# The end of a mixture of experts: three last experts that write their own outputs, and a last norm that holds fewer slots

## The chip, the cores and the metric

The kernel runs on one core of a Trainium2 chip. The core has a matrix engine (PE), a vector engine (DVE), a scalar engine (ACT), GpSimd (POOL), and a sync engine (SP) that here only issues DMA transfers; POOL issues DMA too, the indirect ones (gathers and scatters by a list of rows), in a queue of its own. The engines run side by side, each through its own list of instructions in order, and wait for each other by semaphores. The metric is the device time of one launch in microseconds.

## The reference

One decoder layer, in float32, on 1024 tokens of 1024 channels: a token mixing (sparse attention and RWKV-7, merged), a cross-attention into 256 memory rows, and a grouped mixture of experts, each followed by a LayerNorm of `alpha * x + y`. Only the last part is touched, and the norms:

```
group = argmax over 4 groups of the sum of the two best scores in it
e_idx = the two best of the 4 experts of that group          # per token
gate  = their scores over the scores' sum
y     = sum over the token's two experts of gate * (silu(x @ w_gate[e]) * (x @ w_up[e])) @ w_down[e]
x     = layer_norm(alpha * x + y, ln3_g, ln3_b)               # eps 1e-5
```

There are 16 experts with `w_gate` and `w_up` of 1024 x 512 and `w_down` of 512 x 1024. With the given inputs an expert has between 108 and 160 tokens.

## The kernel before, in words

Up to about 1418 us of the profiled execution the kernel does the token mixing, the cross-attention and the router. Then come the experts, to about 1877 us.

**Products.** A float32 product is made of three: operands are split into a high part (`whi`, `exh`, `ehh`, made by ACT as a cast) and a low part (`wlo`, `exl`, `ehl`, the difference, made by DVE, for one weight chunk of four by POOL); then high x high, low x high and high x low are summed (`k.mm3`, L35 to L37). An expert's weights are six pieces of 1 MB: two of gate, of up, of down. A piece is loaded into one of six raw slots by SP (`load`, L1508), and its parts take one of six high and one of six low slots, all in rotation (`piece`).

**Lists.** The router writes, per expert, a list of slots: a token to read, a row to add to, a gate. The experts are ordered by their number of tokens; in this order the first eight have a main block of 128 slots and a remainder block of 64, the others a main block alone. An empty slot reads token 0 with gate 0, and adds to one of the 128 dump rows that follow the 1024 tokens' rows of the sum. A remainder's list is read twice, onto both halves of the partitions (`rows(..., twice=True)`).

**An expert** (`expert`, a generator whose stages `run` interleaves). Tokens are gathered by POOL (`gather`, L1540, `exg`), transposed by PE (`turned`, L1547, `etp`), and split. Then come gate (`w(0)`), up (`w(1)`) and down (`w(2)`), 24 matmuls of 512 columns each (down's in two halves of 12). A remainder's 64 tokens have high and low part side by side in the stationary operand (`exr`, `ehr`), so that they cost 16 matmuls more in each of gate, up and down (L1580, L1628, L1629), 16 small ones that add the halves and transpose (`etq`, L1599), and transposes of their own. The output goes through ACT (gate as scale, `ey`) and POOL adds its rows to the sum in DRAM (`accd`, `result`, L1621): one indirect transfer with add for a main block, two for a remainder. These transfers are in one order: an add waits for the add before it.

**The end.** The last `LATE` experts don't leave their tokens' outputs to others: each gathers the rows of the sum at its tokens (`z`, L1540 with `src=acc`), adds its own result (L1618), normalizes (`self.ln(z)`) and scatters it to the output (L1624), besides adding to the sum. Ahead of them, `tiles` (L1750ff) makes all 1024 outputs from the sum so far: it loads eight tiles of 128 tokens (L1757), takes moments (by DVE, L967 and L968, or by ACT, L961 and L962), 1/deviation on POOL (L969 or L963 adds eps, L970 raises to -1/2), scales and shifts (L976 and L981 on DVE, or L978 on ACT and L979 on POOL) and writes (L1763). The tiles take `HOLD` raw slots, two tiles each, and these slots hold no weights any more (`self.held`). Late outputs overwrite those of the tiles; the transfers to the output follow each other.

**Order.** `run` opens the experts in a mixed order: two with a remainder, then alternately one without and one with, then the rest without. A scheduler that works on a timeline of estimated durations sets each engine's order from the order of the program, which counts as priority. Steps in a row of the loop in `run` (L1709ff) belong to three experts: the tokens and gate of n, the down of n - 1, the tokens of n + 1.

Nothing follows but the loop `rest` for experts with more tokens than slots, which has no turn with these inputs.

Of the kernel before, what the change touches and what calls it, by code (L numbers as in the profile page):

```python
# [57 lines left out]
def load_xT(k, pool, ps, xin, ident, xh, xl, nt=NT, tag="xraw", bufs=3, pt=(("tp", 2),)):  # L58
    """four token tiles at a time: their loads, then their transposes"""
# [22 lines left out]
class Inproj:  # L82
    """x @ w_in; every consumer's layout goes to DRAM scratch."""
# [40 lines left out]
    # weights stationary, channels on the partitions  # L124
# [5 lines left out]
    def halves(self, wh, wl, evac, tag=None, marks=()):  # L130
        """a half of the tokens at a time"""
# [15 lines left out]
    def tokens(self, x, w, nh):  # L147
        """four token tiles by channels, from channels by tokens"""
        tp = self.bank(nh, "iptp")
        for i in range(4):  # L150
            self.k.nc.tensor.transpose(tp[:, w * i:w * i + w], x[:, 128 * i:128 * i + 128], self.ident[:w, :w])
        return tp[:, :4 * w]
# [112 lines left out]
def t5_onehot():  # L265
    """bucket of distance 1023 - i, one-hot (columns past distance 0 stay empty)"""
# [11 lines left out]
def bias_rows(k, pool, ev, ps, skew):  # L278
    """the bias by distance in DRAM, a copy for every partition; read with rows one place shorter, row p starts p places earlier"""
# [16 lines left out]
class Tables:  # L296
    """bias tables by distance: tb[p, h, c]: distance p + 896 - c; tcm: the compressed keys'; the window's far edge"""
# [24 lines left out]
def compress(k, cst, pool, ps):  # L322
    """k_cmp (twice on the partitions, in parts) and v_cmp (tokens on the partitions, in parts)"""
# [68 lines left out]
class Nsa:  # L392
    def __init__(self, k, cst, dp, skew, ps, keep, right):
        """first loads and the compressed branch's keys and values; ps: a pool with banks for that; keep: opens a pool that stays"""
# [33 lines left out]
    def load(self, t, g, half):  # L428
        """by halves of the tokens"""
# [10 lines left out]
    def attention(self):  # L440
# [6 lines left out]
        with tc.tile_pool(name="nq", reuse_waits="tile", bufs=1) as self.pq, tc.tile_pool(name="nw", reuse_waits="tile", bufs=2) as pw, tc.tile_pool(name="np", reuse_waits="tile", bufs=2, space=PSUM) as ps:  # L447
            def front(br, g, qt, t, st):
                """scores, softmax and gates of one tile of 128 queries of a group"""
# [28 lines left out]
            def weights(g, qt, sums, bs):  # L478
                """the gates over the sums"""
# [7 lines left out]
            def compressed(g, qt, t, st):  # L487
                """scores, softmax and gates against the compressed keys, four heads at once"""
# [20 lines left out]
            def back(g, qt, t, st):  # L509
                """all three branches into one sum: channels of four heads by queries"""  # L510
# [37 lines left out]
            def mix(a, na, b, nb):  # L548
                """steps of a among the first ones of b"""
# [71 lines left out]
class Rwkv:  # L621
    """RWKV-7 in chunks of 64 tokens; an item is a pair of heads and half of the tokens.

    Per chunk, with c the running sum of the log decay: al = e^{c_prev} kk, be = e^{-c} kk a, ka = e^{-c} k, rho = e^{c} r;
# [607 lines left out]
NREM = 8  # L1232
# [228 lines left out]
class Experts:  # L1461
# [193 lines left out]
    def run(self, px, ps):  # L1655
# [50 lines left out]
        for n in range(NE + 1):  # L1706
# [10 lines left out]
            if n + 2 < NE:  # L1717
                open_(n + 2)
# [183 lines left out]
```

## Time and profile before

| what | us |
| --- | --- |
| median of 3 runs | 1899.67 (1896.10 to 1902.39) |
| profiled execution, its span | 1889.9, mean granted clock 0.966 of full |
| experts, from their first gather to the last DVE instruction | about 1424 to 1877 |
| last remainder matmul ends | about 1815 |
| last matmul ends | about 1862 |
| last scatter issued | 1878.5 |
| end of the span | 1889.9 |

The profiled execution's span runs from its first to its last instruction; the median is of the whole launch, of other executions, and 9.8 us larger. In the rows below a busy time is the sum of an engine's instructions; bracketed times are idle time ahead of an instruction, with what ended it. PE's records overlap each other (a matmul of 512 columns is shown with 0.40 us, and one starts every 0.23 us).

### The profile page before, as it was taken

Reading aid. Unit: us, or ns where it says so; the run is one execution under the profiler, and the core shown is the slowest. Engines: PE = TensorE matmul, PEld = TensorE weight load, DVE = VectorE, ACT = ScalarE, POOL = GpSimd, SP = SyncE. Lnnn points to the kernel's source line nnn. Section 1 sums busy time; section 2 is a strip of 40 time slices with the busy share of each in tenths; the row PEclk is TensorE's granted clock in tenths of the full one; section 3 lists DMA queues with packets and bytes.
Section 4 is the critical chain, followed back from the end, with each engine's and each line's share of the span. In section 5 each row is a group of like instructions: output and inputs, shape, how many; then the busy total and the mean of one; then the engine's idle time right before and its main releaser. Section 6 shows DMA issues by size and latency. Waiting matters only on the chain. (4 is left out here: it accounts for less than half of the span.)

```text
span 1889.9 us, 27421 instructions
## 1 busy us (share of the span) xinstructions
PE 1763.5 (93%) x9206; PEld 1433.0 (76%) x9206; DVE 1323.7 (70%) x2774; ACT 849.3 (45%) x1742; POOL 670.3 (35%) x756
## 2 busy tenths in 40 slices
PE   8999999999999999999999899999998999999992
PEld 6877777777788887877888577878796887787771
DVE  3225886888887512498987675557888788788876
ACT  4223313434333222287876341034415676666662
POOL 1123202221222122155445122100356665666556
PEclk9999999999999999999999999999989999999996
DMA  7363343444332227702101774033326999899984
GB/s 232 110 186 106 116 162 113 140 122 126 101 113 84 67 89 231 256 9 82 40 9 32 236 221 167 23 98 126 137 84 246 310 331 289 278 295 292 320 269 143
DMA packets 246144, 302.00 MB, mean 160 GB/s; under 512 B 54653, under 2 KB 142741, under 8 KB 245488
## 3 DMA queue, kind: packets, MB, share of 16 engines
q1 hardware_dynamic: 238016, 273.59, 44.7%
q0 software_dynamic: 7984, 26.62, 5.7%
q8 instruction: 74, 1.21, 0.3%
q14 instruction: 70, 0.57, 0.1%
HBM read 234.05 MB, written 70.98 MB: 161 GB/s over the span
## 5 line engine op out<-in xcount | busy, mean ns | idle before, releaser
L1518 DVE TENSOR_TENSOR wlo<-wraw,whi 128x512 fp32r<-128x512 f32 x288 | 274.5, 1000 | 34.9 <-ACT whi L1517 33.9
L35 PE MATMUL acc<-xh,wh 128*128 128x512 f32 (+1 forms) x656 | 273.0, 416 | 5.2 <-ACT wh L117 3.0
L37 PE MATMUL acc<-xh,wl 128*128 128x512 f32 (+1 forms) x656 | 267.0, 408 | 0.1
L36 PE MATMUL acc<-xl,wh 128*128 128x512 f32 (+1 forms) x656 | 267.1, 408 | 0.0
L1517 ACT CAST whi<-wraw 128x512 fp32r<-128x512 f32 x384 | 207.4, 621 | 36.5 <-PE eacc L1580 10.1
L118 POOL TENSOR_TENSOR wl<-wraw,wh 128x1024 fp32r<-128x1024 f32 (+1 forms) x41 | 104.0, 2536 | 304.1 <-ACT wh L117 259.8
L35 PEld LDWEIGHTS acc<-xh,wh 128*128 128x128 f32 (+1 forms) x656 | 125.0, 191 | 44.0 <-issue 6.8
L1518 POOL TENSOR_TENSOR wlo<-wraw,whi 128x512 fp32r<-128x512 f32 x96 | 138.8, 1476 | 49.4 <-ACT whi L1517 38.1
L37 PEld LDWEIGHTS acc<-xh,wl 128*128 128x128 f32 (+1 forms) x656 | 124.8, 190 | 33.8 <-issue 5.1
L36 PEld LDWEIGHTS acc<-xl,wh 128*128 128x128 f32 (+1 forms) x656 | 125.2, 191 | 30.0 <-issue 3.2
L840 DVE TENSOR_TENSOR tinv<-xinv,ln 128x248 f32<-128x248 f32 (+30 forms) x248 | 85.5, 345 | 40.5 <-DMA ln<-ld 24.3
L28 DVE TENSOR_TENSOR pl<-ptp,ph 128x512 fp32r<-128x512 f32 (+1 forms) x148 | 98.3, 681 | 11.6 <-ACT ph L28 11.1
L470 ACT ACTIVATE pp<-pp,nm 128x640 f32<-128x640 f32 (+7 forms) x128 | 94.2, 738 | 16.4 <-DVE nm L469 15.6
L28 ACT CAST ph<-ptp 128x512 fp32r<-128x512 f32 (+1 forms) x148 | 84.7, 582 | 26.6 <-PE ptp L523 23.6
L36 PE MATMUL eacc<-wlo,exh 128*128 128x512 f32 x240 | 94.2, 393 | 0.4 <-DVE wlo L1518 0.4
L35 PE MATMUL eacc<-whi,exh 128*128 128x512 f32 x240 | 94.3, 393 | 0.0
L37 PE MATMUL eacc<-whi,exl 128*128 128x512 f32 x240 | 94.1, 392 | 0.0
L841 DVE TENSOR_TENSOR xinv<-xinv,tinv 128x248 f32<-128x248 f32 (+30 forms) x248 | 87.6, 353 | 5.9
L475 POOL TENSOR_SCALAR pp<-pp,wgt 128x640 f32<-128x640 f32 (+7 forms) x128 | 88.9, 717 | 1.0
L969 POOL TENSOR_SCALAR lnrs<-lnmv 128x1 f32<-128x1 f32 x21 | 19.6, 934 | 181.0 <-DVE lnmv L968 173.1
L523 PE MATMUL ptp<-ident,pp 128*128 128x128 f32 x528 | 82.1, 278 | 0.3 <-DVE pl L28 0.3
L117 ACT CAST wh<-wraw 128x1024 fp32r<-128x1024 f32 (+1 forms) x41 | 42.2, 1030 | 81.8 <-PE acc L36 44.4
(498 smaller groups left out, 4476.2 us busy)
## 6 DMA issues: line engine op xcount, KB each, us to landing
wraw<-in_moe_w_up SPq DMA_DIRECT2D x32, 1024.0 KB
wraw<-in_moe_w_gate SPq DMA_DIRECT2D x32, 1024.0 KB
wraw<-in_moe_w_down SPq DMA_DIRECT2D x32, 1024.0 KB
wraw<-in_w_in SPq DMA_DIRECT2D x40, 512.0 KB
sm<-ev SPq DMA_DIRECT2D x32, 256.0 KB
sr<-ev SPq DMA_DIRECT2D x28, 256.0 KB
skew<-skew SPq DMA_DIRECT2D x1, 4608.0 KB
xraw<-in_x SPq DMA_DIRECT2D x8, 512.0 KB
```

What stands on the lines that cost most here:

```text
L28: x = nc.scalar.copy(hi, src), nc.vector.tensor_tensor(lo, src, hi.bitcast(F32), ALU.subtract)
L35: nc.tensor.matmul(out, ah, bh, start=start, stop=False)
L36: nc.tensor.matmul(out, ah, bl, start=False, stop=False)
L37: nc.tensor.matmul(out, al, bh, start=False, stop=stop)
L118: nc.gpsimd.tensor_tensor(wl, raw, wh.bitcast(F32), ALU.subtract)
L470: nc.scalar.activation(pt[:, :n], pt[:, :n], AF.Exp, bias=nm, scale=-1.0, accum_out=sums[:, 0, i:i + 1])
L475: nc.gpsimd.tensor_scalar(st[br, i][:, :n], st[br, i][:, :n], w[:, 0, i:i + 1], 1.0, ALU.mult, ALU.mult)
L523: nc.tensor.transpose(tp[:r, 128 * i:128 * i + 128], src, ident)
L840: nc.vector.tensor_tensor(tmp[:, :, :w], x[:, :, j:j + 1].to_broadcast([128, 8, w]), ln[:, j:j + 1, j + 1:].to_broadcast([128, 8, w]), ALU ...
L841: nc.vector.tensor_tensor(x[:, :, j + 1:], x[:, :, j + 1:], tmp[:, :, :w], ALU.subtract)
L1517: nc.scalar.copy(hi[:, cs], raw[:, cs])
L1518: (nc.gpsimd if i in LOPOOL else nc.vector).tensor_tensor(lo[:, cs], raw[:, cs], hi[:, cs].bitcast(F32), ALU.subtract)
```

## The change

Six edits:

- `LATE` goes from 2 to 3: the last three experts write their tokens' outputs themselves, and `tiles` runs one step of the loop earlier. The order of the experts changes with it, in its places 12 to 13: 0 1 8 2 9 3 10 4 11 5 12 6 13 7 14 15 becomes 0 1 8 2 9 3 10 4 11 5 12 6 7 13 14 15 (the numbers are ranks, those below 8 have a remainder).
- `HOLD` goes from 4 to 3: the tiles have six buffers instead of eight, so tiles 6 and 7 take tile 0's and tile 1's; three raw slots instead of two are left to weights.
- From step n = 14 of the loop on, the steps have a higher priority (`PRIO`, 400).
- A remainder's gather fetches 64 rows instead of 128, into a tile (`xgr`) that is made once and whose other 64 rows are set to zero once. The norm's gain is later kept in the same tile.
- The adds to the sum get a bound: a row number above 1023, which is what an empty slot has, is not added.
- The addition of eps in the norms whose moments DVE makes moves from POOL to DVE.

```
-LATE = 2
+LATE = 3
-HOLD = 4
+HOLD = 3
+PRIO = 400
...
             for i in range(2):
                 nc.vector.bn_stats(st[:, i, :], x[:, 512 * i:512 * i + 512])
             nc.vector.bn_aggr(mv, st)
-            nc.gpsimd.tensor_scalar(rs, mv[:, 1:2], self.eps, None, ALU.add)
-        nc.gpsimd.tensor_tensor(rs, rs, self.mh, ALU.pow)
+            nc.vector.tensor_scalar(rs, mv[:, 1:2], self.eps, None, ALU.add)
+            nc.gpsimd.tensor_tensor(rs, rs, self.mh, ALU.pow)
...
     def gather(self, px, ix, tag, src=None):
-        xg = px.tile([128, D], F32, tag="xg" + tag, bufs=2 if tag == "m" else 1, name="exg")
+        if tag == "r":
+            self.k.nc.gpsimd.indirect_dma_start(out=self.xgr[0:64, :], out_offset=None, in_=self.x2d, in_offset=bass.IndirectOffsetOnAxis(ap=ix[0:64, 0:1], axis=0))
+            return self.xgr
+        xg = px.tile([128, D], F32, tag="xg" + tag, bufs=2, name="exg")
...
-                nc.gpsimd.indirect_dma_start(out=self.acc, ..., in_=y[r, :], in_offset=None, compute_op=ALU.add)
+                nc.gpsimd.indirect_dma_start(out=self.acc, ..., in_=y[r, :], in_offset=None, compute_op=ALU.add, bounds_check=T - 1, oob_is_err=False)
...
+        self.xgr = px.tile([128, D], F32, name="xgr")
+        nc.gpsimd.memset(self.xgr[64:128, :], 0.0)
         open_(0)
...
             if n == NE - LATE + 1:
                 row = lambda tag: px.tile([128, D], F32, tag=tag, bufs=1, name="e" + tag)
-                self.norm(self.pl, row("xgr"), row("exr"), [row("gr"), row("yr")])
+                self.norm(self.pl, self.xgr, row("exr"), [row("gr"), row("yr")])
...
-            step(n - 1)
-            step(n + 1)
-            if n + 2 < NE:
-                open_(n + 2)
-            step(n)
-            if n + 1 < NE:
-                gather(n + 1, 1)
+            with self.k.tc.high_priority(offset=PRIO) if n > NE - LATE else ExitStack():
+                step(n - 1)
+                step(n + 1)
+                if n + 2 < NE:
+                    open_(n + 2)
+                step(n)
+                if n + 1 < NE:
+                    gather(n + 1, 1)
```

What stands on the engines moves with it. First PE, from the split of the twelfth expert's hidden part (`etp<-ident,eth`, 1746.56 us in the trace) to the last remainder matmul. Before, with two further experts' hidden parts between:

```order
L1547 MATMUL etp_17043<-ident_111,eth_16763 128x128 x4
L1599 MATMUL etq_17070<-ii_11906,egr_16781 128x64 x8
...
L1547 MATMUL etp_17331<-ident_111,eth_17038 128x128 x4
L1547 MATMUL etp_17390<-ident_111,exg_17185 128x128 x4
...
L1547 MATMUL etp_17562<-ident_111,eth_17292 128x128 x4
L1599 MATMUL etq_17593<-ii_11906,egr_17310 128x64 x8
...
L1629 MATMUL eacc_17650<-wlo_17447,ehr_17606 128x512
```

And after, in the same place of the program, with one:

```order
L1552 MATMUL etp_17084<-ident_111,xgr_13750 128x128 x4
L1552 MATMUL etp_17091<-ident_111,xgr_13750 128x128 x4
L1552 MATMUL etp_17119<-ident_111,eth_16812 128x128 x4
...
L1604 MATMUL etq_17146<-ii_11906,egr_16830 128x64 x6
...
L1552 MATMUL etp_17395<-ident_111,eth_17080 128x128 x4
L1604 MATMUL etq_17422<-ii_11906,egr_17098 128x64 x8
...
L1634 MATMUL eacc_17481<-wlo_17280,ehr_17435 128x512
```

From the first `etp<-ident,eth` of these rows to the last row there are 232 matmuls of 512 columns before and 160 after. The main blocks of three experts follow instead of two.

Second SP, the end of its list before: the last pieces of weights (`wraw<-in_moe_w_...`), the tiles of the sum (`wraw<-accd`) and their outputs.

```order
L1508 DMA wraw_17528<-in_moe_w_up 128x4x512
...
L1508 DMA wraw_17530<-in_moe_w_up 128x4x512
...
L1508 DMA wraw_17589<-in_moe_w_down 128x4x512
...
L1508 DMA wraw_17591<-in_moe_w_down 128x4x512
L1757 DMA wraw_17780<-accd_11904 128x1024 x2
L1757 DMA wraw_17781<-accd_11904 128x1024 x2
L1757 DMA wraw_17782<-accd_11904 128x1024 x2
L1757 DMA wraw_17783<-accd_11904 128x1024 x2
L1763 DMA out_0<-wraw_17780 128x1024
```

And after (L1510 is `load`, L1768 the tiles' loads, L1774 their outputs):

```order
L1768 DMA wraw_17656<-accd_11904 128x1024 x2
...
L1510 DMA wraw_17776<-in_moe_w_up 128x4x512
...
L1510 DMA wraw_17863<-in_moe_w_up 128x4x512
L1774 DMA out_0<-wraw_17654 128x1024
...
L1510 DMA wraw_17865<-in_moe_w_down 128x4x512
L1768 DMA wraw_17654<-accd_11904 128x1024
...
L1774 DMA out_0<-wraw_17656 128x1024 x2
L1774 DMA out_0<-wraw_17654 128x1024 x2
...
L1510 DMA wraw_17913<-in_moe_w_down 128x4x512
```

Before, all weights are asked for ahead of the tiles; after, four pieces stand behind the first tiles' loads, and the last piece behind all outputs, as its slot is one of the tiles'.

Third DVE, the end of its list before: the last two tiles' second passes (L981), and the two late experts' outputs (`exg_17904`, `exg_17986`).

```order
L981 SCALAR_TENSOR_TENSOR wraw_17783<-wraw_17783,lnrs_17860,eexr_17773 128x1024
L976 SCALAR_TENSOR_TENSOR exg_17904<-exg_17904,lnmv_17937,exgr_17772 128x1024
L1618 SCALAR_TENSOR_TENSOR exg_17986<-eacc_17988,ef_17427,exg_17986 128x512
L1618 SCALAR_TENSOR_TENSOR exg_17986<-eacc_18003,ef_17427,exg_17986 128x512
L967 BN_STATS lnst_18021<-exg_17986 128x6
L981 SCALAR_TENSOR_TENSOR exg_17904<-exg_17904,lnrs_17938,eexr_17773 128x1024
```

And after, with the last tile's pass (`wraw_17654`), the first late expert (`exg_17779`), the second (`exg_17973`), and the low part of the last piece (`wlo_17963`):

```order
L982 SCALAR_TENSOR_TENSOR wraw_17654<-wraw_17654,lnrs_17733,eexr_17647 128x1024
L982 SCALAR_TENSOR_TENSOR exg_17779<-exg_17779,lnrs_17815,eexr_17647 128x1024
L1623 SCALAR_TENSOR_TENSOR exg_17973<-eacc_17975,ef_17260,exg_17973 128x512
...
L977 SCALAR_TENSOR_TENSOR exg_17973<-exg_17973,lnmv_18008,xgr_13750 128x1024
L982 SCALAR_TENSOR_TENSOR exg_17973<-exg_17973,lnrs_18009,eexr_17647 128x1024
L1520 TENSOR_TENSOR wlo_17963<-wraw_17913,whi_17962 128x512 x3
L1623 SCALAR_TENSOR_TENSOR exg_18057<-eacc_18059,ef_17536,exg_18057 128x512
```

Before, the weights' low parts end ahead of the tiles' passes; after, they are mixed with them, and the last piece's stand between the second late expert's output and the third's.

## Rows read from the trace of the kernel before

**Rows 1.** the page, busy time of each engine, share of the span, instructions
```profile
PE 1763.5 (93%) x9206; PEld 1433.0 (76%) x9206; DVE 1323.7 (70%) x2774; ACT 849.3 (45%) x1742; POOL 670.3 (35%) x756
```

**Rows 2.** windows: length, busy (instructions) of PE, PEld, DVE, ACT, POOL; clock, DMA, GB/s
```profile
1762.00:1815.00 53.00, 52.07 (x249) 42.68 (x248) 43.38 (x53) 36.60 (x70) 28.11 (x28) 1.00 1.00 326
...
1815.00:1877.00 62.00, 33.98 (x128) 25.80 (x126) 53.05 (x56) 31.20 (x54) 44.26 (x37) 0.78 0.62 192
...
1813.60:1829.20 15.60, 14.87 (x67) 12.03 (x66) 14.37 (x14) 12.35 (x24) 8.74 (x6) 1.00 0.48 85
...
1829.20:1877.00 47.80, 20.51 (x68) 14.91 (x66) 39.98 (x44) 20.25 (x33) 35.81 (x31) 0.71 0.68 230
...
1877.00:1889.90 12.90, 0.00 (x0) 0.00 (x0) 0.00 (x0) 0.00 (x0) 1.08 (x1) 0.50 0.10 37
```

**Rows 3.** timeline of PE: start, length, instruction, count, in brackets the idle time before
```profile
1428.32 1.97 PE L1547 MATMUL etp<-ident,exg 128*128 128x128 f32 x8 [5.01 <-DMA exg<-x2d,eix]
...
1746.56 0.60 PE L1547 MATMUL etp<-ident,eth 128*128 128x128 f32 x4
...
1814.27 0.40 PE L1628 MATMUL eacc<-whi,ehr 128*128 128x512 f32 x1
...
1814.50 0.40 PE L1629 MATMUL eacc<-wlo,ehr 128*128 128x512 f32 x1
```

**Rows 4.** timeline of DVE in the tail
```profile
1815.18 7.53 DVE L1518 TENSOR_TENSOR wlo<-wraw,whi 128x512 fp32r<-128x512 f32 x6 [0.27 <-ACT whi L1517]
...
1834.51 1.29 DVE L967 BATCH_NORM_STATS2 lnst<-wraw 128x6 f32<-128x512 f32 x2 [6.25 <-DMA wraw<-accd]
...
1838.81 2.45 DVE L1518 TENSOR_TENSOR wlo<-wraw,whi 128x512 fp32r<-128x512 f32 x4
...
1873.35 1.29 DVE L976 SCALAR_TENSOR_TENSOR exg<-exg,lnmv,exgr 128x1024 f32<-128x1024 f32 x1
...
1875.41 1.28 DVE L981 SCALAR_TENSOR_TENSOR exg<-exg,lnrs,eexr 128x1024 f32<-128x1024 f32 x1 [0.77 <-POOL lnrs L970]
```

**Rows 5.** timeline of POOL, the last scatters
```profile
1872.75 1.04 POOL L1624 DMA_INDIRECT out<-exg,eix  x1 [0.83 <-DVE exg L981]
...
1878.52 1.08 POOL L1624 DMA_INDIRECT out<-exg,eix  x1 [3.15 <-DMA out<-exg,eix]
```

**Rows 6.** waits of PE, 1417 to 1832 us: total us, times, longest
```profile
PE etp L1547 <- DMA exg<-x2d,eix: 13.7, 4, 5.0
```

**Rows 7.** tile out, 1840 to 1890 us: from a write's issue to its landing
```profile
DMA to landing us min/median/max: 3.4/4.2/5.0
```

**Rows 8.** lines of POOL, 1813.6 to 1877 us: count, busy us, mean ns, idle before
```profile
L979 POOL TENSOR_TENSOR wraw<-wraw,eexr 128x1024 f32<-128x1024 f32 x4 | 11.4, 2856 | 0.7 <-ACT wraw L978 0.7
...
L1518 POOL TENSOR_TENSOR wlo<-wraw,whi 128x512 fp32r<-128x512 f32 x6 | 9.1, 1523 | 3.2 <-ACT whi L1517 3.1
...
L969 POOL TENSOR_SCALAR lnrs<-lnmv 128x1 f32<-128x1 f32 x5 | 4.1, 813 | 7.0 <-DVE lnmv L968 6.9
```

**Rows 9.** timeline of DVE, a small operation of the router
```profile
1401.91 0.17 DVE L1381 TENSOR_SCALAR den<-den 128x3 f32<-128x3 f32 x1
```

**Rows 10.** lines of DVE, 1813.6 to 1877 us
```profile
L1518 DVE TENSOR_TENSOR wlo<-wraw,whi 128x512 fp32r<-128x512 f32 x18 | 17.0, 996 | 1.1 <-ACT whi L1517 1.1
...
L976 DVE SCALAR_TENSOR_TENSOR wraw<-wraw,lnmv,exgr 128x1024 f32<-128x1024 f32 x8 | 13.8, 1752 | 0.0
...
L1618 DVE SCALAR_TENSOR_TENSOR exg<-eacc,ef,exg 128x512 f32<-128x512 f32 x4 | 2.9, 739 | 0.0
...
L967 DVE BATCH_NORM_STATS2 lnst<-exg 128x6 f32<-128x512 f32 x4 | 2.7, 680 | 0.0
...
L1590 DVE SCALAR_TENSOR_TENSOR eth<-eth,eacc 128x512 f32<-128x512 f32 x2 | 1.4, 680 | 0.0
```

**Rows 11.** chain of waits behind the end: start, length, what
```profile
1824.35 4.85 DMA accd<-ey,eix
...
1830.28 8.03 DMA wraw<-accd
```

More of the change, by code (lines that the diff above doesn't have):

```diff
@@ L968, in moments @@
             nc.vector.bn_aggr(mv, st)
-            nc.gpsimd.tensor_scalar(rs, mv[:, 1:2], self.eps, None, ALU.add)
-        nc.gpsimd.tensor_tensor(rs, rs, self.mh, ALU.pow)
+            nc.vector.tensor_scalar(rs, mv[:, 1:2], self.eps, None, ALU.add)
+            nc.gpsimd.tensor_tensor(rs, rs, self.mh, ALU.pow)
         return mv[:, 0:1], ALU.add if by_act else ALU.subtract, rs
@@ L1620, in result @@
                 ix = x[0][0:r.stop - r.start, 1:2]
-                nc.gpsimd.indirect_dma_start(out=self.acc, out_offset=bass.IndirectOffsetOnAxis(ap=ix, axis=0), in_=y[r, :], in_offset=None, compute_op=ALU.add)
+                nc.gpsimd.indirect_dma_start(out=self.acc, out_offset=bass.IndirectOffsetOnAxis(ap=ix, axis=0), in_=y[r, :], in_offset=None, compute_op=ALU.add, bounds_check=T - 1, oob_is_err=False)
             if late:
```

## The prediction

> **What bounds the kernel now.** I read the page's busy shares first, then the stretches of the experts, then what the matrix engine (PE) waits for, then the engines' own orders of time in the last 75 us, and last the chain of waits behind the end. PE is busy 93% of the span [rows 1]. In the experts' stage it is the bound: from 1762 to 1815 us it works 52.07 us of 53, at full granted clock, with the DMA engines busy throughout [rows 2]. The end is different. From 1815 to 1877 PE works only 33.98 us of 62, while VectorE (DVE) works 53.05 us [rows 2]. So two regimes meet at about 1815 us, which I call point M: the end of the last remainder matmul (the row at 1814.50 [rows 3]). Up to M a matmul that goes is time that goes; behind M the DVE's list sets the end. DVE's last instruction ends at 1876.7 [rows 4], the last scatter is issued at 1878.52 because it waits for the scatter ahead of it [rows 5], and 11.4 us later the span is over (1889.9). The profiled execution's 1889.9 us stand 9.8 us below the median of 1899.67 us; I take the differences in the former and add them to the latter.
>
> **Up to M.** Three edits act here.
>
> Halved gathers: the one PE wait that is large is for gathered tokens, 13.7 us in four waits, the largest the first one, 5.01 us, ahead of the first remainder [rows 3, 6]. The remainder's gather now fetches 64 rows instead of 128. A landing is not proportional to bytes (an output write of one tile lands in 3.4 to 5.0 us [rows 7]), so I take 1 us for the first wait and 1.5 us for the other three together, -2.5 us, with ends of 0 and -13.7. By the Trainium skill, "DMA: Bandwidth & Descriptors", section "Anatomy of one DMA — SWDGE (gpsimd) path", a transfer costs a fixed part of 2.0 us and the bytes over 436 GB/s; an estimate by that is 0.6 us less for 256 KB less, so under 1 us a gather; no row here has a gather of half the size.
>
> Dropped rows: on these inputs, 944 of the 3072 added rows are those of empty slots, counted from the reference's routing (1968 of 2048 main slots and 80 of 512 remainder slots are filled). The adds are off PE's path: they run in the software queue, and PE's largest wait is for gathers, not for adds [rows 6]. I cost it at nothing; if the smaller traffic quickens weight pieces, the wait it could shorten is none of PE's.
>
> Norms' addition from POOL to DVE: POOL's took 0.81 us each in the tail [rows 8], the nearest DVE instruction of a few columns 0.17 us [rows 9]. In ln1 and ln2 other operations end each tile, so I count nothing, with ends of -1 and +1. The one-time clearing of 64 rows of the new tile is queued on POOL ahead of its first list, where POOL waits for that list; nothing.
>
> **The order of the experts.** The two last remainder experts become neighbours, and an expert without remainder moves behind them. Between the transposes at 1746.56 and M before has 232 matmuls of 512 columns; after has 160 (the rows of the order show both ends). At 0.23 us from one to the next [rows 3] the 72 are 16.6 us, with 12 fewer 128-column transposes at 0.15 us each (0.60 us for four [rows 3]) 18.4 us. The stretch also has some 6 us in which PE waits (68.3 us long, less 62.2 us: 232 x 0.233, 44 transposes and 16 small products). M moves from 1814.9 to 1796 with these and to about 1791 without; as only one of these waits is for a remainder's own gather, I take 1793. These 72 matmuls are not saved but come behind M, beside DVE work.
>
> **Behind M.** DVE starts 1.3 us ahead of M (1813.6), so at 1791.7. Its list from there in before is 14.37 + 39.98 = 54.35 us [rows 2]. After has on top: one expert's six pieces of weights, three low parts on DVE each, 18 x 0.996 = 17.9 us [rows 10]; two products of the gate, one split of the hidden part, two of the tokens, 5 x 0.68 = 3.4 us [rows 10]; and a third expert's output: 2 x 0.739 + 2 x 0.68 + 0.20 + 1.3 for the first and 1.27 for the second pass of the norm + 6 additions of 0.17 = 6.6 us [rows 4, 9, 10]. The first pass is taken at the 1.29 us that it takes where POOL is quiet [rows 4]; the mean of such passes in the tail is 1.75 us [rows 10]. The sum is 82.2 us.
>
> Its idle time: before waited 6.25 us for the tiles of the sum to come in [rows 4], after the last adds (4.85 us) and the loads (8.03 us) [rows 11]. That wait now falls where DVE has low parts to make, so it goes. What is late next is the last piece of weights: with three slots held by tiles, its load stands at the end of SP's queue behind all eight output writes, as its slot is a tile's. Let t0 be the start of the last tile's last DVE pass. Then 1.3 us for it, 4.2 for its write to land [rows 7], 5 for the piece (estimate between 4.2 and 8.0), 3.2 for its four casts and the low parts behind them (estimate, five steps of the 0.61 us that a low part takes alone [rows 4]), 1.5 for the last matmuls (six at 0.23), 4.5 for the last expert's half sum, statistics and passes (0.74 + 0.68 + 0.20 + 0.17 + 1.29 + 1.27): 19.7 us, of which DVE has 15 us of other work, so 4.7 us idle at least. DVE ends at 1791.7 + 82.2 + 4.7 = 1878.6 and the last scatter follows 0.3 us later: it no longer waits for an earlier one, as the two others are issued long before. That is 1878.9 against 1878.52: +0.4 us. With the -2.5 us from ahead of M the sum is -2.1 us: 1897.5 us.
>
> The unknown sizes: M at 1791 or 1796 (-2 to +3); the added low parts at 0.61 us (2.45 us for four while POOL is quiet) or at 1.26 us (7.53 us for six while POOL makes its own) [rows 4], -7 to +4.7; idle 0 to 10. The first two ends partly exclude each other, since a DVE list that is shorter makes the wait for the last piece longer.
>
> **Priority.** It only changes which ready instruction goes first behind M. It can't shorten DVE's list; it is in the order that I have priced.
>
> **Rivals.**
> A, faster: PE's gather waits vanish, since the remainder's gathers stand earlier in POOL's order and are half as long. Of 13.7 us, 10.7 lie ahead of 1746 us (the fourth is within the stretch of the order), and a quicker M adds 2. For it: four waits are all that PE has in 400 us. Against: only the first is ahead of a remainder by its row [rows 3], and the DMA engines are busy throughout [rows 2]. Time: 1897.5 - 8.2 - 2 = about 1887 us.
> B, slower: the two element-wise engines get in each other's way in a tail that now has more of both. The rows show 0.61 us for a low part alone and 1.26 us beside POOL's [rows 4]; POOL's own take 1.52 us, and its passes over a tile 2.86 us [rows 8]. All 18 added low parts at 1.26 us cost 4.7 us more than in the sum and the third norm's first pass 1 us; and as the last piece waits for the last tile, t0 shifts by the same amount. It decides if t0 falls later than 1878.6 - 19.7 = 1858.9 us; each us beyond is one at the end. At t0 of 1866 us the time is 1897.5 + 7 = about 1905 us. The Trainium skill, "GPSIMD Engine Reference", section "Specifications", says that GpSimd's SBUF interfaces are shared with VectorE, with contention at DVE instructions with two SBUF inputs; by that rule every low part, and every pass of the norm over a tile, is such an instruction. The trace agrees for the low parts, which take twice as long there.
> C, the change doesn't do what it says: dropped rows and half gathers move no wait at all, since POOL's instructions and landings stay as many. Then only the tail counts: +0.4, 1900 us, with the same uncertainty.
>
> **How the numbers follow.** This kernel's runs can tell 0.3%, 5.7 us, from no change. The forecast with its own range (1892 to 1904) has 0.46, C 0.14, A 0.22, B 0.18. Of the forecast and C some 0.16 lies past -5.7 us (short low parts) and 0.04 past +5.7; of A 0.20 and of B 0.17 lie past it. Faster 0.36, slower 0.21, same 0.43. The range is 1884 to 1907: A's time with 3 us beyond, B's with 2.
>
> **What would show it.** PE's total wait for gathered tokens between 1417 and 1832 falls by 1 to 4 us; if it falls by 10, A. The last remainder matmul ends near 1793, less what is gained ahead of it. DVE's first low part behind that point to its last pass is 82 us busy; if above 88, B. The last piece's load is issued after the last tile's write, at about 1863. The last scatter no longer waits for another. It is wrong if PE, not DVE, ends the tail, if a wait of PE in the experts' middle appears that was not there, or if adds now hold POOL back: the first late expert's add must wait until all eight tiles are read, and the low parts queued behind it on POOL wait with it.

## The result and the profile after

The changed kernel takes 1911.94 us (median of 18 runs, 1902.88 to 1917.81) against 1898.72 us of the kernel before on the same chip (18 runs, 1892.77 to 1906.77). The ratio is 1.0066, with a 95% interval of 1.0052 to 1.0080: slower by 13 us. I had forecast 1897.5 us, within 1884 to 1907.

The page of the changed kernel, busy time of each engine, as in [rows 1]; and its software queue (packets, MB, share of 16 engines):

```profile
PE 1774.2 (93%) x9206; PEld 1440.0 (75%) x9206; DVE 1324.4 (69%) x2803; ACT 849.2 (44%) x1742; POOL 668.0 (35%) x739
...
q0 software_dynamic: 7760, 21.68, 4.6%
```

The number of matmuls is that of before. The queue of gathers, adds and scatters carries 21.68 MB; in the kernel before it was this:

```profile
q0 software_dynamic: 7984, 26.62, 5.7%
```

So less is moved, as dropped rows and halved gathers ask for. The stretches, answering to [rows 2] (length, busy time and count of PE, PEld, DVE, ACT, POOL; clock, DMA, GB/s):

```profile
1762.00:1815.00 53.00, 50.98 (x254) 42.26 (x253) 35.34 (x49) 33.86 (x66) 26.32 (x29) 1.00 0.87 274
1815.00:1877.00 62.00, 42.63 (x171) 32.50 (x169) 62.00 (x68) 39.31 (x70) 46.67 (x35) 0.82 0.68 239
1809.20:1900.90 91.70, 58.50 (x218) 43.72 (x216) 81.12 (x94) 48.66 (x87) 59.73 (x47) 0.77 0.67 213
1877.00:1913.00 36.00, 10.07 (x22) 6.43 (x22) 14.02 (x21) 3.55 (x6) 10.89 (x9) 0.55 0.47 125
```

From 1815 to 1877 DVE has no gap at all (62.00 of 62; before 53.05). Behind 1877, where the kernel before has 12.9 us left, in which only the last scatter is issued and lands, there are 36 us, in which every engine is idle most of the time: DVE works 14.02 us. Where they go is in the timeline of all engines from the last tile's last DVE pass (1872.87, what the prediction called t0) on; start, length, instruction, idle time before it (a name with q, as `SPq`, is that engine's sequencer):

```profile
1872.72 2.35 POOL L980 TENSOR_TENSOR wraw<-wraw,eexr 128x1024 f32<-128x1024 f32 x1
1872.87 3.29 DVE L982 SCALAR_TENSOR_TENSOR wraw<-wraw,lnrs,eexr 128x1024 f32<-128x1024 f32 x1
...
1876.08 1.27 DVE L982 SCALAR_TENSOR_TENSOR exg<-exg,lnrs,eexr 128x1024 f32<-128x1024 f32 x1
...
1879.17 0.40 SPq L1510 DMA_DIRECT2D wraw<-in_moe_w_down  x1
...
1879.99 1.01 POOL L1629 DMA_INDIRECT out<-exg,eix  x1 [2.35 <-SPq L1745]
...
1887.34 2.18 ACT L1519 CAST whi<-wraw 128x512 fp32r<-128x512 f32 x4 [3.38 <-SPq L1745]
1887.98 1.29 DVE L1520 TENSOR_TENSOR wlo<-wraw,whi 128x512 fp32r<-128x512 f32 x2 [4.15 <-ACT whi L1519]
...
1888.48 1.11 POOL L1545 DMA_INDIRECT exg<-accd,eix  x1 [5.97 <-DMA out<-exg,eix]
...
1889.89 1.23 POOL L1629 DMA_INDIRECT out<-exg,eix  x1 [0.30 <-issue]
...
1891.12 1.30 POOL L1520 TENSOR_TENSOR wlo<-wraw,whi 128x512 fp32r<-128x512 f32 x1
...
1892.48 0.80 PE L36 MATMUL eacc<-wlo,ehh 128*128 128x512 f32 x1 [0.82 <-POOL wlo L1520]
...
1893.02 0.75 DVE L1623 SCALAR_TENSOR_TENSOR exg<-eacc,ef,exg 128x512 f32<-128x512 f32 x1 [2.78 <-DMA exg<-accd,eix]
...
1894.35 0.63 PE L37 MATMUL eacc<-whi,ehl 128*128 128x512 f32 x1
...
1899.30 1.28 DVE L982 SCALAR_TENSOR_TENSOR exg<-exg,lnrs,eexr 128x1024 f32<-128x1024 f32 x1 [0.46 <-POOL lnrs L971]
1900.88 1.04 POOL L1629 DMA_INDIRECT out<-exg,eix  x1 [1.61 <-DVEq L1745]
```

The last piece of weights is asked for at 1879.17, behind the last tile's write, and its first cast comes 8.2 us later. Four casts follow, three low parts on DVE, and the fourth low part on POOL, which stands there behind a gather that had waited 5.97 us and a scatter. Then come the last matmuls, to 1895.0, the last expert's additions and norm, and at 1900.88 the last scatter, which waits for no other scatter (before, 3.15 us [rows 5]).

Two landmarks divide the run: the first hidden part's transpose, at 1449.43 us before and here at 1465.95, and point M, which answers to 1814.50 of [rows 3]:

```profile
1465.95 0.60 PE L1552 MATMUL etp<-ident,eth 128*128 128x128 f32 x4
...
1810.12 0.40 PE L1634 MATMUL eacc<-wlo,ehr 128*128 128x512 f32 x1
```

From these rows of every kernel I made the table on which the rest stands. "Middle" is from the first hidden part to M, "tail" from M to the last scatter's issue.

| kernel | late | bound on adds | first hidden part at | middle | tail | span |
| --- | --- | --- | --- | --- | --- | --- |
| before | 2 | no | 1449.4 | 365.5 | 63.6 | 1889.9 |
| before, again | 2 | no | 1452.9 | 358.2 | 61.7 | 1884.2 |
| halved gathers alone | 2 | no | 1463.5 | 367.1 | 61.0 | 1903.0 |
| late 2, all rows | 2 | no | 1458.6 | 362.6 | 63.1 | 1895.7 |
| bound alone | 2 | yes | 1453.5 | 356.3 | 58.9 | 1880.2 |
| bound and eps | 2 | yes | 1465.7 | 353.0 | 58.8 | 1888.9 |
| late 2 | 2 | yes | 1470.0 | 362.8 | 59.1 | 1903.2 |
| late 2, again | 2 | yes | 1458.7 | 353.5 | 58.9 | 1882.5 |
| changed | 3 | yes | 1466.0 | 344.6 | 90.4 | 1913.4 |
| no eps | 3 | yes | 1465.1 | 344.3 | 93.9 | 1915.5 |
| no priority | 3 | yes | 1467.8 | 336.0 | 93.0 | 1908.7 |
| own z | 3 | yes | 1463.6 | 335.0 | 90.1 | 1900.9 |
| hold 4 | 3 | yes | 1467.4 | 341.1 | 86.2 | 1906.8 |
| hold 4 and own z | 3 | yes | 1463.2 | 338.2 | 83.5 | 1897.1 |

Each is one execution; within a group the tails lie up to 4 us apart, the middles up to 10. The means are 363.4 and 62.4 for the four with two late experts and all rows, 356.4 and 58.9 for the four with the bound, 340.0 and 91.9 for changed, no eps, no priority and own z. So on the means the bound takes 10.5 us from the two together (7.0 and 3.5); the middles of the first two groups overlap, the tails don't. The third late expert takes 16.4 from the middle and adds 33.0 to the tail, a loss of 16.6 us, of which the bound's gain covers the larger part.

### The profile page after: what moved, and what is told of

It reads as the page before. It is cut to its first block, busy times and chain, and to the rows that moved or that the text cites. A ratio compares the mean times of both kernels' runs of the same rounds, so it can differ in the third digit from the quotient of the medians.

```text
span 1913.4 us, 27464 instructions
## 1 busy us (share of the span) xinstructions
PE 1774.2 (93%) x9206; PEld 1440.0 (75%) x9206; DVE 1324.4 (69%) x2803; ACT 849.2 (44%) x1742; POOL 668.0 (35%) x739
## 3 DMA queue, kind: packets, MB, share of 16 engines
q0 software_dynamic: 7760, 21.68, 4.6%
## 5 line engine op out<-in xcount | busy, mean ns | idle before, releaser
L1520 DVE TENSOR_TENSOR wlo<-wraw,whi 128x512 fp32r<-128x512 f32 x288 | 266.7, 971 | 39.3 <-ACT whi L1519 37.4
L1520 POOL TENSOR_TENSOR wlo<-wraw,whi 128x512 fp32r<-128x512 f32 x96 | 135.8, 1449 | 51.1 <-ACT whi L1519 45.9
L470 ACT ACTIVATE pp<-pp,nm 128x640 f32<-128x640 f32 (+7 forms) x128 | 94.2, 738 | 16.8 <-DVE nm L469 16.0
L898 ACT COPY state<-rseq 64x64 f32<-64x64 f32 x128 | 26.6, 208 | 118.6 <-PE rseq L894 99.5
L117 ACT CAST wh<-wraw 128x1024 fp32r<-128x1024 f32 (+1 forms) x41 | 42.2, 1030 | 78.9 <-PE acc L36 37.1
```

The costliest lines, as they stand in the source:

```text
L470: nc.scalar.activation(pt[:, :n], pt[:, :n], AF.Exp, bias=nm, scale=-1.0, accum_out=sums[:, 0, i:i + 1])
L1520: (nc.gpsimd if i in LOPOOL else nc.vector).tensor_tensor(lo[:, cs], raw[:, cs], hi[:, cs].bitcast(F32), ALU.subtract)
```

## The experiments

Every ratio is against runs of the kernel before on the same chip. It is not the quotient of two medians, and the experiments ran on three chips, so kernels are to be compared by their ratios and not by their microseconds.

**What the third late expert costs.** The changed kernel with two late experts, four held slots and no priority, everything else kept. It was run twice, the second time beside the single edits below.

```
-HOLD = 3
+HOLD = 4
...
-LATE = 3
+LATE = 2
...
-            with self.k.tc.high_priority(offset=PRIO) if n > NE - LATE else ExitStack():
+            with ExitStack():
```

> The changed kernel with two late experts, four slots held, no priority and the old order of experts: it keeps only the halved gathers, the bounded adds and the eps addition on DVE. Theory T (the tail: the last piece of weights behind the tiles' outputs, a chain of some 28 us from the last tile's last pass to the last scatter where 19.7 were priced): the loss goes, 1895 to 1898 us against 1898.7 before, ratio 0.998 to 1.000. Rival H (the loss lies ahead of the experts, where the changed profile is 15 us later when the first remainder is transposed): it stays, 1904 to 1912 us, ratio above 1.003.

> The first experiment's kernel once more (two late experts, four slots, old order; halved gathers, bound and eps), beside its parts on one chip. Theory T: ratio 0.995 to 0.999 again, so the third late expert and what comes with it carry more than the whole loss. If it is at 1.000 or above, the loss is less than shown in the first experiment by as much.

Measured: 1893.30 us, ratio 0.9970 (0.9944 to 0.9996), and again 1885.36 us, 0.9957 (0.9936 to 0.9977). The loss is gone, and what remains of the change is a gain. Against the changed kernel's 1.0066 the third late expert with its slots and priority costs about 1%, 18 to 21 us.

**What the rest is worth.** The same without the bound (late 2, all rows); and the kernel before with one or two of the edits: the bound alone, the halved gathers alone, the bound and the eps.

```
-    ... in_=y[r, :], in_offset=None, compute_op=ALU.add, bounds_check=T - 1, oob_is_err=False)
+    ... in_=y[r, :], in_offset=None, compute_op=ALU.add)
```

> The kernel with two late experts, four slots held and the old order, as in the first experiment, and without the bound of the adds: rows of empty slots are added again. If the dropped rows shorten the adds' landing, the way from the last remainder matmul to the last scatter grows from 59.0 us to 61 or more, towards the 63.6 of the kernel before, and the time by 2 to 4 us, 1895 to 1897. If they cost nothing, as predicted: 1893 us and 59 us.

> The kernel before with the bound of the adds alone: rows of empty slots are not added. The two kernels with two late experts differ by this bound and by 0.7% (1893 us with it, 1902 without). If the dropped rows are worth that by themselves: 1888 to 1892 us, ratio 0.994 to 0.997, and 58 to 60 us from the last remainder matmul to the last scatter (61.7 and 63.6 in the two profiles of the kernel before). If they cost nothing, as predicted: ratio 0.999 to 1.001.

> The kernel before with the halved gathers of the remainders alone (64 rows into one tile that stays, its other half cleared once). Predicted: -2.5 us, ratio 0.998 to 1.000. Against it: the kernel with these and the eps addition on DVE, without the bound, took 0.4% more than the kernel before; if the gathers cause that, ratio 1.002 to 1.006, with more waiting of PE for gathered tokens or a later start of the experts.

> The kernel before with the bound of the adds and the eps addition on DVE, without the halved gathers. Predicted for the eps: 0. If so it equals the kernel with the bound alone within 3 us. If the eps addition costs what the kernel without the bound showed too much: 4 to 8 us above it.

Measured: late 2 with all rows 1902.17 us, 1.0041 (1.0019 to 1.0063); the bound alone 1885.37 us, 0.9959 (0.9941 to 0.9977); halved gathers alone 1897.65 us, 1.0019 (0.9996 to 1.0042); bound and eps 1884.39 us, 0.9951 (0.9931 to 0.9971). Late 2 again and late 2 with all rows differ by the bound alone, 0.9957 against 1.0041, though on two chips. So the bound is worth 0.4% alone and 0.8% there; the runs don't say why it is more there. What is good in the change is the bound; alone, or with eps, which adds nothing measurable, it beats both kernels. The halved gathers gain nothing: 1.0019 lies between the two forms of its expectation and decides for neither, and late 2 with all rows, which is the kernel before with halved gathers and eps, is slower than it. The adds and the gather behind them on POOL, kernel with the bound alone:

```profile
1806.20 1.61 POOL L1621 DMA_INDIRECT accd<-ey,eix  x1 [3.24 <-ACT ey L1616]
1814.33 1.43 POOL L1621 DMA_INDIRECT accd<-ey,eix  x1 [0.42 <-issue]
1817.28 1.67 POOL L1621 DMA_INDIRECT accd<-ey,eix  x1 [0.19 <-ACT whi L1517]
1820.49 1.20 POOL L1540 DMA_INDIRECT exg<-accd,eix  x1 [0.23 <-DMA accd<-ey,eix]
```

and the same places before:

```profile
1811.25 1.61 POOL L1621 DMA_INDIRECT accd<-ey,eix  x1 [3.24 <-ACT ey L1616]
1819.13 1.69 POOL L1621 DMA_INDIRECT accd<-ey,eix  x1 [0.16 <-issue]
1824.35 1.46 POOL L1621 DMA_INDIRECT accd<-ey,eix  x1 [2.20 <-DMA accd<-ey,eix]
1829.46 0.99 POOL L1540 DMA_INDIRECT exg<-accd,eix  x1 [2.36 <-DMA accd<-ey,eix]
```

Before, add waits for add and the gather for the last add, 2.20 and 2.36 us; with the bound the order is the same, but the next add waits for none and the gather 0.23 us. From M (1809.8 there, 1814.9 before) to the gather it is 10.7 us instead of 14.6, and DVE's wait for the tiles of the sum, 6.25 us in [rows 4], is now this:

```profile
1823.95 1.29 DVE L967 BATCH_NORM_STATS2 lnst<-wraw 128x6 f32<-128x512 f32 x2 [0.72 <-DMA wraw<-accd]
```

The wait is 5.3, 5.0 and 6.6 us in the other three kernels of the first group (before again, halved gathers alone, late 2 with all rows) and 1.8, 1.8 and 0.9 us in the other three with the bound (bound and eps, late 2, late 2 again): it goes with the dropped rows. The landings of the adds (tile `accd`, 1425 to 1818 us), before, with halved gathers alone, with the bound alone, and with bound and eps:

```profile
DMA to landing us min/median/max: 4.9/8.3/10.9
```

```profile
DMA to landing us min/median/max: 5.8/8.7/11.1
```

```profile
DMA to landing us min/median/max: 2.7/7.2/10.7
```

```profile
DMA to landing us min/median/max: 4.5/7.0/10.9
```

The two kernels with all rows have medians of 8.3 and 8.7 us, the two with the bound 7.2 and 7.0. The middle is shorter too, by 7.0 us on the means; through which waits the runs don't show.

**eps and priority in the changed kernel.** One undone at a time.

```
-            nc.vector.tensor_scalar(rs, mv[:, 1:2], self.eps, None, ALU.add)
+            nc.gpsimd.tensor_scalar(rs, mv[:, 1:2], self.eps, None, ALU.add)
```

> The changed kernel with the eps addition back on POOL. Theory T: no change from the changed kernel within 3 us (1909 to 1914 us). Rival H, in the form that the norms' addition on DVE delays ln1, ln2 and the router: 6 us or more less, 1906 us or below.

Measured: 1909.57 us, 1.0059 (1.0034 to 1.0083), no difference from 1.0066.

```
-            with self.k.tc.high_priority(offset=PRIO) if n > NE - LATE else ExitStack():
+            with ExitStack():
```

> The changed kernel without the priority of the last steps. By the prediction the priority only orders ready work: the same time within 3 us, 1909 to 1915. The last piece is asked for at the same place of SP's list, so the chain from the last tile's last pass to the last scatter stays at 28 us within 2.

Measured: 1912.21 us, 1.0096 (1.0067 to 1.0125) from four runs. It overlaps 1.0066 (1.0052 to 1.0080); if the priority does anything, it helps. The second half of the expectation failed: in this profile the chain from the last tile's last pass (1872.46) to the last scatter (1896.75) is 24.3 us, not 28, and the last piece has its first cast 5.0 us after it was asked for. The tail is no shorter for it (93.0 us), since that pass starts 68.7 us after M, not 62.4.

**What ends the tail.** Two waits stand near its end: the last piece of weights and the last expert's gather of the sum, which waits 5.97 us because its buffer (two for this tag) is the first late expert's, whose scatter must land first. "Own z" gives that gather a buffer of another tag (tag "z" is passed for the last expert alone); "hold 4" gives the tiles four slots again, so that the last piece's slot is not the last tile's; the third kernel has both.

```
-        xg = px.tile([128, D], F32, tag="xg" + tag, bufs=2, name="exg")
+        xg = px.tile([128, D], F32, tag="exh" if tag == "z" else "xg" + tag, bufs=2, name="exg")
...
-HOLD = 3
+HOLD = 4
```

> The changed kernel with a buffer of its own for the last expert's rows of the sum, so that their gather waits no longer for the first late expert's scatter (a wait of 5.97 us on POOL in the changed profile). If that wait ends the tail: 5 us less than the changed kernel. Theory T (the last piece's chain ends 2 to 3 us later than the gather): 0 to 2 us less; the gather's wait goes from the profile all the same, and POOL's low part of the last piece comes earlier by up to 2 us.

> The changed kernel with eight tile buffers again (four slots held, two left to weights): tiles 6 and 7 wait for no output, the first late add comes some 20 us earlier, and the last piece needs only tile 0's and 1's slot. Theory T: the end of the chain is no longer tied to the last tile's output, 5 to 10 us less than the changed kernel, 1902 to 1907 us. Rival B (the low parts and passes on DVE and POOL get in each other's way): the same work on both engines, so the same time, 1909 to 1914 us.

> The changed kernel with four slots held and with a buffer of its own for the last expert's rows of the sum: neither the last piece waits for the last tile's output nor the last gather for the first late scatter. Theory T: DVE's list alone ends the tail then, 82 to 84 us from 1.3 us ahead of the last remainder matmul to the last scatter (86.2 us in the kernel with four slots held alone, 90.4 in the changed one), 1899 to 1903 us: still not below the kernel before, since the list is longer by what PE gains. Rival B: POOL and DVE stretch each other, 88 us and more, 1906 us.

Measured: own z 1905.29 us, 1.0047 (1.0025 to 1.0069); hold 4 1906.50 us, 1.0030 (0.9998 to 1.0061); both 1900.45 us, 1.0032 (1.0013 to 1.0051). In own z the gather waits no more, and the tail is as long as before it (90.1 us against 90.4):

```profile
1867.18 0.40 SPq L1510 DMA_DIRECT2D wraw<-in_moe_w_down  x1
...
1870.92 1.83 POOL L1545 DMA_INDIRECT exg<-accd,eix  x1 [0.40 <-DMA accd<-ey,eix]
...
1877.20 2.18 ACT L1519 CAST whi<-wraw 128x512 fp32r<-128x512 f32 x4 [4.67 <-SPq L1745]
...
1888.72 1.04 POOL L1629 DMA_INDIRECT out<-exg,eix  x1 [1.61 <-DVEq L1745]
```

There the last piece ends it, 10.0 us from issue to first cast instead of 8.2; from that cast to the end of the last matmul it is 5.6 us instead of 7.6, as POOL's low part starts 2.2 us after the cast and not 3.8. So the gather's wait did cost something, and the slower piece hides it. With hold 4 the piece is asked for ahead of the last tiles' writes, the tail is 86.2 us, and the gather's wait is what ends it:

```profile
1862.08 0.40 SPq L1510 DMA_DIRECT2D wraw<-in_moe_w_down  x1
...
1870.29 2.16 ACT L1519 CAST whi<-wraw 128x512 fp32r<-128x512 f32 x4
...
1883.03 1.85 POOL L1545 DMA_INDIRECT exg<-accd,eix  x1 [0.36 <-DMA out<-exg,eix]
...
1888.24 0.75 DVE L1623 SCALAR_TENSOR_TENSOR exg<-eacc,ef,exg 128x512 f32<-128x512 f32 x1 [4.25 <-DMA exg<-accd,eix]
```

So two chains of nearly one length seem to lie behind each other: against the changed kernel's profile, the tail without the gather's wait is as long, without the piece's place 4.2 us shorter, without both 6.9 us (83.5). Each is one execution, and tails of a group lie up to 4 us apart, so only the 6.9 us stand clear. The first late add comes 31.7 us after M with hold 4 and 47.0 in the changed kernel, 15 us earlier where I had expected some 20. With both waits off, DVE's list is the bound; the window from 1.3 us ahead of M to the last scatter, with both:

```profile
1800.10:1884.90 84.80, 56.20 (x218) 42.38 (x216) 79.90 (x94) 48.66 (x86) 62.52 (x47) 0.83 0.72 231
```

DVE works 79.90 of 84.80 us. In late 2 again the same window is 60.2 us:

```profile
1810.90:1871.10 60.20, 33.84 (x134) 26.08 (x132) 55.50 (x63) 32.80 (x57) 43.55 (x33) 0.79 0.59 192
```

The third late expert brings 24.4 us of DVE work (79.90 - 55.50) behind M, and takes 16.4 us of PE work from ahead of it. With both waits off the tail is still 24.6 us longer (83.5 - 58.9), so that 8 us are lost, and the timing agrees in sign: 1.0032 against 0.9957, intervals apart.

**The kernel before once more**, for a second profile of it.

> The kernel before, unchanged, profiled once more, to see what of the changed profile's 15 us ahead of the experts is the change's. Theory T: the way from the start to the first expert's hidden part varies by that much from execution to execution (1449.4 us in the first profile, 1463 to 1470 in five profiles of changed kernels, of which one has the norms as before): 1455 us or later here. Rival H: 1450 us again. From there to the last scatter it should be 429 us as in the first profile, within 5.

Measured: 1886.10 us, one run. PE's waits for gathered tokens between 1417 and 1832 us, 13.7 us in [rows 6], are 7.4 us in it, with no edit at all. Neither form of the expectation came: the first hidden part starts at 1452.9 us, between the 1450 and the 1455 that I had set, and from there to the last scatter it is 419.9 us, 9 less than in the first profile.

## Why the prediction was wrong, step by step

**In short.** The forecast was 2.1 us less than before, the measurement is 13 us more. The step that failed is the one that put the third late expert at +0.4 us, by two of its terms. The chain behind t0 was priced at 19.7 us and took 27.7, so that the tail is 90.4 us instead of 85.9. And the wait of 6.25 us for the tiles of the sum was credited to the third late expert, while the dropped rows, costed at nothing, take it away without it. The 2.5 us from the halved gathers did not come either. The runs show in their place that the third late expert with its order, slots and priority costs 18 to 21 us (1.0066 against 0.9970 and 0.9957), of which the stages hold 16.6, and that the bound gives about 8 back. Where the rest lies is open (at the end of this section).

**The dropped rows, "I cost it at nothing": wrong, and the largest error of reasoning.** The bound by itself is worth 0.41% (0.9959), 8 us. I had argued from PE's waits alone. But the rows I showed had DVE waiting 6.25 us behind the last adds and the tiles' loads [rows 4, 11], and that chain starts with an add's landing, which shorter adds shorten. I gave this wait's disappearance to the third late expert, as one of its gains. With the bound alone, and two late experts, it is 0.72 us. So the third late expert has to be paid for without it.

**The chain behind t0, "19.7 us": 27.7 us (and 0.3 to the scatter).** By its parts, predicted and measured: the pass 1.3 and 3.3 (POOL's pass of 2.35 us runs beside it); the write until the piece is issued 4.2 and 3.0; the piece, until its first cast, 5 and 8.2; casts and low parts 3.2 and 5.1 (1887.34 to 1892.42; the fourth low part is POOL's, and I had priced five equal steps without asking what POOL has queued); the last matmuls 1.5 and 2.6; the last expert 4.5 (its six terms add to 4.35) and 5.6. The piece was bounded at 8.0 in the prediction and taken at 5; 5.0, 8.0, 8.2 and 10.0 us are the values of no priority, no eps, changed and own z, so 5 was the quick end and not the middle. t0 itself came early: 62.4 us after M, where I needed it no later than 65.9 (1858.9 - 1793). So the tail is 90.4 us instead of 85.9.

The matmuls' part shows what the granted clock is, from 1888 to 1895 us:

```profile
1888.00:1895.00 7.00, 6.16 (x12) 3.60 (x12) 3.42 (x5) 1.51 (x3) 3.63 (x3) 0.50 0.42 141
```

0.50 of full, that is 1.2 GHz, after PE had been idle for 4.77 us; a matmul starts every 0.42 us there, not every 0.23 as in [rows 3].

**Behind M, "82.2 us" of DVE: right.** 81.12 us in the changed kernel, 79.90 with both waits off. Its idle time is 10.6 us (91.70 - 81.12) instead of 4.7, just past the 10 that I allowed at most. What it waits for, from 1.3 us ahead of M to the last scatter (total us, times, longest):

```profile
DVE wlo L1520 <- ACT whi L1519: 5.1, 4, 4.2
DVE exg L1623 <- DMA exg<-accd,eix: 2.8, 1, 2.8
```

The first is the last piece.

**The order of the experts, M 21.9 us earlier: right in the sum, not in the parts.** From the first hidden part M comes 20.9 us earlier (344.6 against 365.5), on the means 23.4. But on the means 7.0 of these are the bound's; the third late expert gives 16.4, close to the 16.6 that I had for the 72 matmuls alone.

**Halved gathers, "-2.5 us": nothing.** 1.0019 (0.9996 to 1.0042) alone. The gather does land earlier (kernel with halved gathers alone, tiles `exg` and `xgr`, 1420 to 1800 us):

```profile
DMA to landing us min/median/max: 4.5/5.8/8.1
```

```profile
DMA to landing us min/median/max: 3.8/5.1/10.5
```

0.7 us in the median, near the estimate of 0.6 by the Trainium skill, "DMA: Bandwidth & Descriptors", section "Anatomy of one DMA — SWDGE (gpsimd) path". PE's waits for gathered tokens in the changed kernel fell by 6.6 us, past the 1 to 4 of the forecast and short of the 10 of rival A (waits of PE, 1417 to 1832 us; the first row is for later):

```profile
PE first L1408 <- issue: 4.9, 9, 1.2
PE etp L1552 <- DMA exg<-x2d,eix: 4.0, 2, 3.0
PE etp L1552 <- DMA xgr<-x2d,eix: 3.1, 1, 3.1
```

7.1 us against 13.7. But the kernel before falls to 7.4 by itself from one profile to the next, and the kernel with halved gathers alone has 10.3: I read a single execution's wait as the kernel's.

**eps on DVE, nothing: right.** Its DVE instruction takes 0.14 to 0.15 us in the tail, a little less than the 0.17 of [rows 9].

**Rival B (element-wise engines in each other's way).** Its signs did not come: DVE is not above 88 us busy, and t0, counted from M, was not late. Its mechanism is there in one link of the chain behind t0, the pass of 3.29 us. By the Trainium skill, "GPSIMD Engine Reference", section "Specifications", such a pass, with two inputs in SBUF, contends with POOL; the trace agrees, and by more than the doubling that I had read from the low parts.

**Rivals A and C.** A needed PE's waits to go; 7.1 us of them are left. C needed that no wait moves; the wait for the tiles of the sum did, by the bound.

**The basis.** I set the profiled 1889.9 us against a median 9.8 higher and carried that over as fixed. A launch takes about 2 us more than its span (1915.44 against 1913.4 in the changed kernel); the rest is spread, since the 18 launches of either kernel lie up to 9 us from their median, and the profiled execution was one of the quicker.

**What stays open.** On the means the middle and tail give +6.1 us from before to changed (-23.4 + 29.5), the timing 13. In the profiles the difference lies ahead of the first hidden part, which starts at 1463 to 1468 us in all six kernels with three late experts and at 1449 and 1453 us before. But the edited kernels with two late experts stand at 1453 to 1470, and that with 1465.7 (bound and eps) was timed as fast as that with 1453.5 (bound alone), so that start may be the execution's and not the kernel's. The traces narrow it down. The changed kernel is 7.0 us later than the one before at the router's first product (1403.55 against 1396.58) and 16.8 us later at the first expert's first matmul (1434.25 against 1417.49). In between PE stands still in ten gaps, 5.1 us in all, that end with no wait that the profile shows ("issue", the first row above has nine of them); before has none. No priority, hold 4, hold 4 and own z, and late 2 have such gaps too (4.3 to 5.7 us), the other nine profiles have none of more than 0.2 us. Late 2 again, without gaps, is the same kernel as late 2, so they can come in one execution and stay away in another. Whether kernels with three late experts have them more often (four of six profiles, against one of eight) the runs don't settle, nor the distance between the stages' 16.6 us for the third late expert and the timing's 21 (1.0066 against 0.9957).

## What to carry to other kernels

Moving work from ahead of a point into a tail pays only by what the tail's bound engine does not get on top: here 16.4 us of PE work left the stretch that PE bounds, and 24.4 us of DVE work came to the one that DVE bounds. A wait that two edits of one change could remove is credited once, and first to the smaller edit; here less data in the adds took it away. For a last load behind a freed slot, follow each link to the end, with what else is queued on every engine that it passes, and add the slow value of each.

## What the runs showed of the hardware

- Indirect adds whose empty slots are dropped by the bound land earlier: median 8.3 and 8.7 us with all rows, 7.0 to 7.2 us with them dropped (three profiles).
- A DVE instruction that reads two tiles in SBUF can take far longer than twice its time beside POOL. The pass at 1872.87 took 3.29 us beside POOL's 2.35 (alone 1.27). A low part, 0.61 us alone [rows 4], took 4.56 us where POOL made a low part and then a pass. Rows of DVE and POOL of the changed kernel:

```profile
1859.63 1.81 POOL L1520 TENSOR_TENSOR wlo<-wraw,whi 128x512 fp32r<-128x512 f32 x1
1859.76 4.56 DVE L1520 TENSOR_TENSOR wlo<-wraw,whi 128x512 fp32r<-128x512 f32 x1
1860.88 2.88 POOL L980 TENSOR_TENSOR wraw<-wraw,eexr 128x1024 f32<-128x1024 f32 x1
```

Both DVE instructions end about their own time alone behind the end of POOL's: 1864.32 against 1863.76, and 1876.16 against 1875.07. The other rows say the same. From 1425 us on, the fourteen profiles have 1030 low parts and passes on DVE that take more than 0.72 us (low part) or 1.48 us (pass). Of these, 937 low parts end 0.54 to 0.56 us, and 57 passes 1.08 to 1.10 us, behind the end of a low part or pass of POOL; the other 36, all low parts, took at most 0.76 us and have none beside them. So in these cases DVE stands until POOL is through and then takes nearly its own time alone, rather than both going at half speed: the six low parts of [rows 4], 1.26 us on the mean, are three of 0.68 us and three of 1.44, 1.69 and 2.66 us. The doubling of the prediction was no rate.
- From the issue of the last 1 MB piece to its first cast it took 8.2, 10.0 and 8.0 us (changed, own z, no eps), with a scatter of a whole tile issued 0.8 us behind it, and 5.0 us in no priority, where the scatter came 1.25 us behind it. No run separates the scatter from other causes.
